# A hybrid layer on one core: second parts of weights on another engine, turns in another order, and another choice of places for expert weights

## The chip, the core and the metric

The kernel runs on one core of a Trainium2 chip. The metric is device time in microseconds (us), the median of several runs. The core has a matrix engine (PE), a vector engine (DVE), an activation engine (ACT), a general engine (POOL) and a queue (SP) from which nearly all transfers (DMAs) are issued. Each engine takes its instructions in the order in which the program holds them. The program here is a manual schedule: the order in which the Python code records instructions is the order on each engine, and a semaphore wait is put wherever one engine needs what another has made or must first have read.

## What is computed

One layer of a diffusion backbone over 512 latent tokens and 256 context tokens, width 1024, in float32. The reference, cut to its core:

```python
h  = modulate(rms_norm(x, w), shift, scale)         # also for the context tokens
u, q, k, v, ga, gb = split_in(h @ w_in)
ya = s5_mixer(uc, u)      # complex diagonal recurrence, both directions
yb = diff_attention(q, concat(kc, k), concat(vc, v))
m  = sigmoid(ga) * (ya @ w_proj_a) + sigmoid(gb) * (yb @ w_proj_b)
x  = x + g_m * rms_norm(m @ w_out, w_post)
h  = modulate(rms_norm(x, w_ffn), ...)
aff = softmax(h @ w_router); gates, idx = top_k(aff.T, 64)     # 16 experts, 64 tokens each
ys  = (silu(xs @ w_gate[e]) * (xs @ w_up[e])) @ w_down[e] * gates
x  = x + g_f * rms_norm(scatter_add(ys), w_post_ffn)
```

The weights of the 16 experts are 402.7 MB of the 467 MB that are moved.

## The kernel before

**Products in two parts.** In the layer's first part a float32 weight is split into two numbers that the PE takes at a higher rate: the first part is a rounded copy that ACT writes, the second part is weight minus first part (`lo`, L246). The PE adds three products per weight tile (`PASSES`): first by first, first by second, second by first. So the third matmul of a tile needs the second part. In the stretch of interest the second parts are subtractions of 128 x 1024 elements, and POOL makes them (`lo(GP, ...)`): by `parts` (L248 to 254) for the weights of u and v, by `prep_gate` (L662 to 671) for the gates ga.

**The recurrence.** The state-space branch runs over chunks. Its serial part is a loop of 95 steps on the DVE (L747 to 756), four small subtensor operations each (L753 to L756), recorded in one piece before any of the gates. While the DVE walks through it, the PE computes the eight gates ga (`gate`, L685; two halves of 12 matmuls each on 512 columns), after each half of gates 2 to 5 one group of "taps" (`taps`, L773: short convolution matrices, PE then ACT, into KS), and then v for the first six of eight weight tiles (`v_some`). Gate n+2's parts are made right after gate n, in one of two buffers (`wsp`); the raw weights come in pairs of gates (`load_gate`). When all taps are there, `mt_load` copies them by 30 small transfers from KS into MT, on the SP queue; behind them in the same queue stand the loads of the raw weights of v's tiles 2 and 3 (`fetch(vraw[p], 1536, p + 2)`). After v the PE computes the readout y (L865 on), which needs the recurrence's last states.

**Ahead of the recurrence** the DVE builds the state matrices (`matrices`, `state_make`, consumed by `ahead(n)`), the PE turns them (`state_turn`, L476), ACT copies the turned ones (WT, L491). The rows of u are turned by the DVE (`u_turn`, L558) through two buffers. Then the DVE builds the readout matrices (`cp_make`, four times five operations of 128 x 1024, L452 to L461).

**Places.** The memory for big tiles is a set of places of 128 x 2048 float32, handed out from a queue `E` (`take`, `give`). In the expert stage a load of 2 MB (`load_w`, L1617) takes from `E` either one whole place of 4096 columns (a pair: P0 to P5, and the first 4096 columns of SR) or two single ones (L places, SR's last part "SR1", and once each U2's and gm's). The P places lie where the front's weights lay, and come free with the last output projection (wo). `room` (L1604 to 1614) picks: the head of `E`; if that is a single one, also the next single one in the queue, wherever it stands. Since all loads go through SP in order, a load whose place is not yet free holds those behind it. An expert is twelve such loads: gate u0 to u3, up u0 to u3, down q0 to q3.

```python
tag = E.popleft()
if is_pair(tag):
    ...
tags = [tag, next(x for x in E if not is_pair(x))]
E.remove(tags[1])
```

Of the kernel before, what the change touches and what calls it, by code (L numbers as in the profile page):

```python
# [33 lines left out]
def layer(ctx: ExitStack, tc: tile.TileContext, A, out):  # L34
# [134 lines left out]
    def exp_exact(o, x, get):  # L169
        sh = list(x.shape)  # L170
        c, k, r, p, ki = get(*sh), get(*sh), get(*sh), get(*sh), get(*sh, dt=I32)
        V.tensor_scalar(c, x, -87.0, 88.0, op0=OP.max, op1=OP.min)
        V.tensor_scalar(k, c, 1.0 / math.log(2.0), MAGIC, op0=OP.mult, op1=OP.add)
        V.tensor_scalar(k, k, MAGIC, None, op0=OP.subtract)
        V.scalar_tensor_tensor(r, k, -LN2H, c, op0=OP.mult, op1=OP.add)
        V.scalar_tensor_tensor(r, k, -LN2L, r, op0=OP.mult, op1=OP.add)
        V.tensor_scalar(ki, k, 127.0, 8388608.0, op0=OP.add, op1=OP.mult)
        V.tensor_scalar(p, r, EXPC[0], None, op0=OP.mult)
        for a in EXPC[1:]:
            V.scalar_tensor_tensor(p, p, a, r, op0=OP.add, op1=OP.mult)  # L180
        V.scalar_tensor_tensor(o, p, 1.0, ki.bitcast(F32), op0=OP.add, op1=OP.mult)
# [63 lines left out]
    def lo(eng, o, a, hi):  # L245
        eng.tensor_tensor(o, a, hi.bitcast(F32), op=OP.subtract)  # L246

    def parts(raw, eng):  # L248

        t = take("wp")  # L250
        hi_, lo_ = t[:, 0:1024].bitcast(F32R), t[:, 1024:2048].bitcast(F32R)
        S.activation(hi_, raw, AF.Copy)
        lo(eng, lo_, raw, hi_)
        return t, [v.rearrange("p (k f) -> p k f", k=2) for v in (hi_, lo_)]

    PASSES = ((0, 0), (0, 1), (1, 0))
# [74 lines left out]
    S.activation(sc, th, AF.Sin)  # L331
    diagonals(0, 4, "rx")
    wu = [parts(wur[0], GP)]
    exp_exact(mag, q1, rowt)
    L = rowt(64, 4, 64)
    V.tensor_tensor(L[:, 0], mag, sc[:, 1], op=OP.mult)
    V.tensor_tensor(L[:, 1], mag, sc[:, 0], op=OP.mult)
    den, nr = rowt(64, 64), rowt(64, 64)
    V.tensor_tensor(den, lre, lre, op=OP.mult)
    V.tensor_tensor(q2, lim, lim, op=OP.mult)  # L340
    V.tensor_tensor(den, den, q2, op=OP.add)
    V.reciprocal(den, den)
    V.tensor_scalar(nr, L[:, 0], 1.0, None, op0=OP.subtract)
    V.tensor_tensor(q1, nr, lre, op=OP.mult)
    V.tensor_tensor(q2, L[:, 1], lim, op=OP.mult)
    V.tensor_tensor(q1, q1, q2, op=OP.add)
    V.tensor_tensor(L[:, 2], q1, den, op=OP.mult)
    V.tensor_tensor(q1, L[:, 1], lre, op=OP.mult)
    V.tensor_tensor(q2, nr, lim, op=OP.mult)
    V.tensor_tensor(q1, q1, q2, op=OP.subtract)  # L350
    V.tensor_tensor(L[:, 3], q1, den, op=OP.mult)
    pp = bank("prmT")
    PE.transpose(pp[:, 0:65], prm, ident[0:65, 0:65])
    prmT = keep.tile([128, 65], F32, name="prmT")

    for k in range(2):
        PE.transpose(pp[:, 128 + 12 * k:140 + 12 * k], prf[:, k::2], ident[0:12, 0:12])
    V.tensor_copy(prmT, pp[:, 0:65])
    prfT = keep.tile([128, 3, 8], F32, name="prfT")
    V.tensor_copy(prfT.rearrange("p v (u k) -> p k v u", k=2), pp[:, 128:152].rearrange("p (k v u) -> p k v u", k=2, v=3))  # L360

    def nb(t):

# [27 lines left out]
    ada_half(0)  # L391
    ada_mod(0)
    hh_ = [[take("hh") for _ in range(2)] for _ in range(2)]
    hh = [[hh_[r][d // 4][:, 512 * (d % 4):512 * (d % 4) + 512].bitcast(F32R) for d in range(8)] for r in range(2)]
    hc_ = [take("hc") for _ in range(2)]
# [230 lines left out]
    ub = ub_.rearrange("p (b g i h) -> p b g i h", b=2, g=G, i=2)  # L626
    u2 = big("U2", "u2").rearrange("p (g c) -> p g c", g=G)
    u_turn(2)
    ahead(4)
    u_turn(4)  # L630
    for kt in range(4, 8):
        u_some(range(2), kt)
    ahead(4)
    u_turn(0)
    give(*(w[0] for w in wu[2:]), ub_, xbc_)
    state_turn(0, 0)
    ahead(5)
    state_turn(1, 0)
    ahead(5)
    state_turn(0, 1)  # L640
# [7 lines left out]


    GW = {}  # L650

    def gate_room(raw):
        GW["raw"], GW["w"], GW["wv"] = raw, [], []
# [10 lines left out]
    def prep_gate(n, eng):  # L664
        if len(GW["w"]) < 2:
            GW["w"].append(take("wsp"))
            GW["wv"].append(GW["w"][-1].rearrange("p (r k f) -> p r k f", r=2, k=8).bitcast(F32R))
        w, c = GW["wv"][n % 2], 128 * (n % GW["k"])
        raw = GW["raw"].rearrange("p (k f) -> p k f", k=8)[:, :, c:c + 128]
        S.activation(w[:, 0], raw, AF.Copy)  # L670
        lo(eng, w[:, 1], raw, w[:, 0])

    def passes(ps, w, x, ks, last):
        for kt in ks:
# [5 lines left out]
    def gate(n, eng, get):  # L680

        sg = sga_ if n < 8 else sgb_
        if n % 4 == 0:
            sg.append(take("sg"))
        w = GW["wv"][n % 2]  # L685
        pg = get("gate")
        passes(pg, w, hh, range(4), 7)
        yield
        passes(pg, w, hh, range(4, 8), 7)
        S.activation(sg[-1][:, 512 * (n % 4):512 * (n % 4) + 512], pg, AF.Tanh, scale=0.5)  # L690
        if n % 8 < 6:
            prep_gate(n + 2, eng)
        if n < 8:
            if n in (1, 3):
                load_gate(n + 3)
        elif n < 13:
            load_gate(n + 3, 1)
        yield
# [2 lines left out]
    graw = take("graw")  # L701
    gate_room(graw)
    load_gate(0)
    prep_gate(0, GP)
    prep_gate(1, GP)
    load_gate(2)
    SR = big("SR", "SR").rearrange("p (c r g) -> p c r g", r=2, g=16)
    for dr in range(2):
        for gq in range(8):
# [14 lines left out]
    for dr in range(2):  # L724
        for gh in range(2):
            cp_make(dr, gh)
    give(mm)
    BZ_ = take("BZ")
    BZ = BZ_.rearrange("p (r g a h) -> p r g a h", r=2, g=32, a=2)
# [14 lines left out]
        cb = 97 + (31 - s if s < 32 else 127 - s)  # L744
        return SR[:, s:cb + 1:cb - s]

    for s in range(1, 96):  # L747
        if s == 32:
            V.tensor_copy(SR[:, 97 + 96], SR[:, 97])
        h0, h1 = rows(s - 1), rows(s)  # L750
        sp = keep.tile([128, 2, 2, 16], F32, name="sp", bufs=2)
        sq = keep.tile([128, 2, 2, 16], F32, name="sq", bufs=2)
        V.tensor_tensor(sp, h0, AR, op=OP.mult)  # L753
        V.tensor_tensor(sq, h0[:, :, ::-1], AI, op=OP.mult)  # L754
        V.tensor_tensor(sp, sp, h1, op=OP.add)
        V.tensor_tensor(h1, sp, sq, op=OP.add)  # L756


    co_ = [0]
# [51 lines left out]
    ft = taps()  # L811
    wv = []
    for n in range(8):
        if n == 7:
            wv += [parts(vraw[p], GP) for p in range(2)]
            for p in range(2):
                fetch(vraw[p], 1536, p + 2)
        for _ in gate(n, GP, cobank):
            if n > 1:
                next(ft, None)  # L820
        if n == 5:
            for _ in ft:
# [26 lines left out]
    for p in range(3):  # L849
        v_some(p, range(6))  # L850
        give(wv[p][0])
        if p < 2:
            wv.append(parts(vraw[p % 2], GP))
    give(vraw_)


    YS_ = take("YS")
# [745 lines left out]

    def room():  # L1604

        tag = E.popleft()
        if is_pair(tag):
            t = wl[:, 0:4096] if tag[0] == "SR" else pr.tile([128, 4096], F32, name="we", tag="P%d" % tag[1])
            return t, [t[:, 0:2048], t[:, 2048:4096]], [tag]
        tags = [tag, next(x for x in E if not is_pair(x))]  # L1610
        E.remove(tags[1])
        return None, [regs.tile([128, 2048], F32, name="wh", tag=x) if isinstance(x, str) else wl[:, 4096:6144] if x[0] == "SR" else
                      gm_ if x[0] == "gm" else yp_.rearrange("p b d -> p (b d)") for x in tags], tags

    def done_w(tags):
        E.extend(x for x in tags if x[0] not in ("U2", "gm"))
# [231 lines left out]
```

## Time and profile before

| | us |
|---|---|
| median of 3 runs | 1612.13 (1611.4 to 1614.61) |
| the profiled execution's own time | 1610.17 |
| its span, first to last instruction | 1608.4 |
| PE busy | 1394.9 (87%) |
| DVE busy | 553.9 (34%) |
| ACT busy | 292.6 (18%) |
| POOL busy | 173.9 (11%) |
| HBM read | 461.66 MB, 288 GB/s over the span |

Busy shares are averages over two unlike stages: the front (to about 640 us), where all engines take part, and the experts (from there on), where PE and transfers run side by side. The chain of waits (part 4 of the profile's page) is followed back from the last instruction; a row of a timeline gives start, length, engine, line, operation, output and inputs, and in brackets how long the engine had stood idle before it and what ended that.

### The profile page before, as it was taken

What the parts mean: (1) busy time and instruction counts of PE and PEld (TensorE: products, weight loads), DVE (VectorE), ACT (ScalarE), POOL (GpSimd) and SP (SyncE); (2) the same over time, 40 slices, a digit from 0 to 9 for tenths busy, and PEclk for the clock granted to TensorE, in tenths of its full rate; (3) what the DMA queues carried; (4) which work ended last, traced back from release to release, by engine and by line L of the source; (5) the groups of instructions that cost most, each with busy time, mean ns of one, the idle gap of its engine ahead of it and who ended that gap; (6) DMA issues with size and microseconds to landing.
All of it is one profiled execution on the core that took longest, in us unless ns stands there. A gap on an engine that the chain in (4) does not pass through costs nothing.

```text
span 1608.4 us, 17710 instructions
## 1 busy us (share of the span) xinstructions
PE 1394.9 (87%) x7230; PEld 745.4 (46%) x7230; DVE 553.9 (34%) x1363; ACT 292.6 (18%) x566; POOL 173.9 (11%) x115
## 2 busy tenths in 40 slices
PE   5989959996997894989988979988989979989984
PEld 3778746874664583424324324324324324324322
DVE  6789952276656637001102102102002002012003
ACT  3572104145442331100000000000000000000002
POOL 2123302443123300000000000000000000000003
PEclk9999979998997896999999999999999999999998
DMA  9112402322444157389999999999999999999994
GB/s 331 38 54 83 76 27 96 92 92 86 154 181 157 34 190 318 127 373 426 426 427 427 426 427 428 425 427 427 427 427 426 427 426 427 428 427 428 426 413 159
DMA packets 76881, 467.01 MB, mean 290 GB/s; under 512 B 13716, under 2 KB 33360, under 8 KB 46432
## 3 DMA queue, kind: packets, MB, share of 16 engines
q1 hardware_dynamic: 75616, 463.62, 71.6%
q10 hardware_dynamic: 768, 2.13, 0.3%
q8 instruction: 57, 0.93, 0.2%
q0 software_dynamic: 416, 0.12, 0.0%
q14 instruction: 24, 0.20, 0.0%
HBM read 461.66 MB, written 2.10 MB: 288 GB/s over the span
## 4 chain that ended last, share of the span: by engine, by line
PE 47%; DMA 30%; DVE 17%; ACT 3%; issue 2%; POOL 0%; SPq 0%; DVEq 0%; ACTq 0%
DMA we<-in_w_exp_up_dram 18%; DMA we<-in_w_exp_down_dram 11%; PE gu L1673 11%; PE yd L1705 8%; PE gat L1643 4%; PE sca L1717 4%; PE wo L1520 3%; PE gate L676 2%; DVE SR L756 2%; PE u L548 2%; DVE sp L753 1%; PE k L1054 1%; PE proj L676 1%; DVE sq L754 1%; PE y L877 1%
## 5 line engine op out<-in xcount | busy, mean ns | idle before, releaser
L1673 PE MATMUL gu<-we,gm 128*64 128x512 f32 x752 | 169.5, 600 | 23.3 <-DMA we<-in_w_exp_up_dram 20.1
L1673 PE MATMUL gu<-we,gf 128*64 128x512 f32 x752 | 169.1, 600 | 22.8 <-DMA we<-in_w_exp_up_dram 18.3
L1684 DVE TENSOR_TENSOR hid<-hid,gu 128x512 f32<-128x512 f32 x32 | 21.9, 688 | 481.1 <-PE gu L1673 481.1
L1705 PE MATMUL yd<-we,hid 128*64 128x512 f32 x688 | 152.9, 595 | 9.4 <-DMA we<-in_w_exp_down_dram 9.4
L1758 POOL TENSOR_TENSOR fin<-facc,gf 128x256 f32<-128x256 f32 (+1 forms) x12 | 10.6, 914 | 1020.0 <-DMA we<-in_w_exp_down_dram 1015.8
L1673 PEld LDWEIGHTS gu<-we,gm 128*64 128x64 f32 x752 | 53.0, 138 | 138.1 <-issue 105.8
L1673 PEld LDWEIGHTS gu<-we,gf 128*64 128x64 f32 x752 | 53.1, 138 | 136.7 <-issue 104.9
L676 PE MATMUL gate<-hh,wsp 128*128 128x512 f32 x384 | 95.8, 403 | 12.4 <-ACT sg L690 12.0
L1705 PEld LDWEIGHTS yd<-we,hid 128*64 128x64 f32 x688 | 48.6, 137 | 106.6 <-issue 91.3
L1710 DVE COPY mo<-yd 64x512 f32<-64x512 f32 x15 | 10.4, 694 | 227.8 <-ACT mo L1709 227.8
L676 PEld LDWEIGHTS gate<-hh,wsp 128*128 128x128 f32 x384 | 71.9, 192 | 29.1 <-ACT sg L690 12.4
L1643 PE MATMUL gat<-mo,x 128*128 128x128 f32 x512 | 71.8, 300 | 10.2 <-DVE mo L1635 10.2
L1643 PEld LDWEIGHTS gat<-mo,x 128*128 128x128 f32 x512 | 67.3, 208 | 18.3 <-issue 15.2
L1681 ACT ACTIVATE hid<-gu 128x512 f32<-128x512 f32 x32 | 19.1, 597 | 297.8 <-PE gu L1673 297.8
L1717 PE MATMUL sca<-mo,gm 128*128 128x512 f32 (+1 forms) x136 | 61.6, 591 | 4.8 <-ACT mo L1709 4.8
L1689 ACT COPY hid<-ht 128x512 f32<-128x512 f32 x16 | 9.4, 587 | 270.5 <-PE ht L1688 270.5
L1520 PE MATMUL wo<-wo,mp 128*128 128x512 f32 x192 | 47.5, 404 | 2.3 <-DVE at L1380 2.3
L1709 ACT ACTIVATE mo<-yd 64x512 f32<-64x512 f32 x15 | 8.9, 590 | 219.0 <-PE yd L1705 219.0
L1722 DVE TENSOR_TENSOR facc<-facc,sca 128x512 f32<-128x512 f32 (+1 forms) x60 | 38.6, 651 | 18.8 <-PE sca L1717 18.7
L1673 PE MATMUL gu<-wl,gm 128*64 128x512 f32 x200 | 45.0, 599 | 0.0
L1717 PEld LDWEIGHTS sca<-mo,gm 128*128 128x128 f32 x136 | 21.5, 188 | 44.4 <-DVE facc L1722 23.6
L1520 PEld LDWEIGHTS wo<-wo,mp 128*128 128x128 f32 x192 | 36.6, 194 | 10.4 <-DVE at L1380 2.8
(439 smaller groups left out, 1985.2 us busy)
## 6 DMA issues: line engine op xcount, KB each, us to landing
we<-in_w_exp_up_dram SPq DMA_DIRECT2D x48, 2048.0 KB, 32.6
we<-in_w_exp_gate_dram SPq DMA_DIRECT2D x46, 2048.0 KB, 34.2
we<-in_w_exp_down_dram SPq DMA_DIRECT2D x43, 2048.0 KB, 26.7
wl<-in_w_exp_gate_dram SPq DMA_DIRECT2D x9, 2048.0 KB, 29.9
araw<-in_w_ada_dram SPq DMA_DIRECT2D x16, 1024.0 KB, 6.3
wl<-in_w_exp_down_dram SPq DMA_DIRECT2D x7, 2048.0 KB, 33.8
wl<-in_w_exp_up_dram SPq DMA_DIRECT2D x7, 2048.0 KB, 26.7
wl<-in_w_exp_down_dram SPq DMA_DIRECT2D x11, 1024.0 KB, 31.9
```

The costliest lines, as they stand in the source:

```text
L548: PE.matmul(ps, tok(a, i, kt), w[b][:, kt % 2], start=kt == first and n == 0, stop=kt == last and n == 2)
L676: PE.matmul(ps, w[:, a, kt], x[b][kt], start=kt == 0 and n == 0, stop=kt == last and n == 2)
L753: V.tensor_tensor(sp, h0, AR, op=OP.mult)
L756: V.tensor_tensor(h1, sp, sq, op=OP.add)
L1520: PE.matmul(po[j], mparts(a, kt)[:, 128 * i:128 * i + 128], wo[kt][:, D * b + 512 * j:D * b + 512 * j + 512].bitcast(F32R), start=kt == 0 ...
L1643: PE.matmul(pg, x1[i][:, nb(d)], oh[:, i].rearrange("p e s -> p (e s)"), start=i == 0, stop=i == 3)
L1673: PE.matmul(pq[b][64 * j:64 * j + 64], xst[e // 2 % 2][:, kt, e % 2], wv[:, c:c + 512], start=kt == 0, stop=kt == 7, skip_group_check=True)
L1681: S.activation(hid[0][:, 1 - e % 2, b], pq[b], AF.Silu)
L1684: V.tensor_tensor(act, act, pgu[1][b], op=OP.mult)
L1705: PE.matmul(py[64 * j:64 * j + 64], hT_[:, b, i, 64 * jf:64 * jf + 64], wv[:, c:c + 512], start=(q == 0 and i == 0), stop=(q == 3 and i == ...
L1717: PE.matmul(po, gm[:, g0:g0 + 128], yp_[:, ep % 2, c], start=True, stop=True)
L1722: V.tensor_tensor(dst, dst, po, op=OP.add)
```

## The change

Four edits. (1) `prep_gate` and `parts` take `None` for the engine: the subtraction then goes into a list `due`, and `second_parts()` records what is in it, on the DVE. The recurrence becomes a generator; `steps(n)` records n of its steps, and the code calls it four steps per half of a gate and ten per tile of v, with `second_parts()` in between. The loads of raw gate weights that must follow a subtraction go into the same list. The fetch of v's raw tiles 2 and 3 moves behind gate 7. (2) `u_turn(4)` stands ahead of the state matrices' next four pieces, and the first state turn ahead of `u_turn(0)`. (3) In the setup the first half of the modulation (`ada_half(0)`, `ada_mod(0)`) stands ahead of the DVE's work on the discretisation, and two small copies go from the DVE to ACT. (4) `room` walks `E` and takes what is complete first: a pair, or the second of two single places.

```diff
         S.activation(hi_, raw, AF.Copy)
-        lo(eng, lo_, raw, hi_)
+        if eng is None:
+            due.append(lambda: lo(V, lo_, raw, hi_))
+        else:
+            lo(eng, lo_, raw, hi_)
...
     u_turn(2)
+    u_turn(4)
     ahead(4)
-    u_turn(4)
     for kt in range(4, 8):
         u_some(range(2), kt)
-    ahead(4)
+    state_turn(0, 0)
+    ahead(2)
     u_turn(0)
     give(*(w[0] for w in wu[2:]), ub_, xbc_)
-    state_turn(0, 0)
-    ahead(5)
+    ahead(7)
...
             if n in (1, 3):
-                load_gate(n + 3)
+                due.append(lambda: load_gate(n + 3))
...
-    prep_gate(0, GP)
-    prep_gate(1, GP)
-    load_gate(2)
+    prep_gate(0, None)
+    prep_gate(1, None)
+    due.append(lambda: load_gate(2))
...
         for gh in range(2):
             cp_make(dr, gh)
+        second_parts()
...
     for n in range(8):
         if n == 7:
-            wv += [parts(vraw[p], GP) for p in range(2)]
+            wv += [parts(vraw[p], None) for p in range(2)]
+        for half, _ in enumerate(gate(n, None, cobank)):
+            steps(4)
+            if half == 0:
+                second_parts()
+            if n > 1:
+                next(ft, None)
+        if n == 7:
             for p in range(2):
                 fetch(vraw[p], 1536, p + 2)
-        for _ in gate(n, GP, cobank):
-            if n > 1:
-                next(ft, None)
...
         if p < 2:
-            wv.append(parts(vraw[p % 2], GP))
+            wv.append(parts(vraw[p % 2], None))
+        steps(5)
+        second_parts()
+        steps(5)
     give(vraw_)
+    steps(95)
...
-        tag = E.popleft()
-        if is_pair(tag):
...
-        tags = [tag, next(x for x in E if not is_pair(x))]
-        E.remove(tags[1])
+        ones_ = []
+        for tag in E:
+            if is_pair(tag):
+                E.remove(tag)
...
+            ones_.append(tag)
+            if len(ones_) == 2:
+                break
```

**On the general engine and the vector engine.** During the first gates POOL's row was this (wsp: a gate's two parts, at gates 2 to 4 here; KS: the taps):

```order
L730 MEMSET BZ 128x2048
L768 TENSOR_TENSOR cn<-ident 32x16
L769 TENSOR_TENSOR cn<-cn,DG 32x256
L246 TENSOR_TENSOR wsp<-graw,wsp 128x1024 x2
L797 TENSOR_TENSOR KS<-KS,cn 32x4x16
L246 TENSOR_TENSOR wsp<-graw,wsp 128x1024
L797 TENSOR_TENSOR KS<-KS,cn 32x4x16 x2
```

It is now the following, and POOL's next subtraction is the one for the readout's gate (wg):

```order
L744 MEMSET BZ 128x2048
L790 TENSOR_TENSOR cn<-ident 32x16
L791 TENSOR_TENSOR cn<-cn,DG 32x256
L819 TENSOR_TENSOR KS<-KS,cn 32x4x16 x4
L246 TENSOR_TENSOR wg<-wgr,wg 128x2048
```

The DVE has the twelve subtractions: those of gates 0 and 1 together between the second and the third `cp_make`, gate 2's behind step 12 of the recurrence, those of gates 3 to 7 behind every eighth step after it, those of v's tiles 0 and 1 behind step 60, tile 2's behind step 69, tile 3's behind step 79. Tile 2's place, in the middle of the steps:

```order
L771 TENSOR_TENSOR SR<-sp,sq 128x2x32
L246 TENSOR_TENSOR wp<-vraw,wp 128x1024
L768 TENSOR_TENSOR sp<-SR,AR 128x64
L769 TENSOR_TENSOR sq<-SR,AI 128x64
L770 TENSOR_TENSOR sp<-sp,SR 128x64
```

What moved: the 26 steps behind it, and all that the DVE does after, now stand behind that one subtraction.

**On the SP queue, the first expert.** Before (wh: a single place; wl: SR's, 4096 the whole pair, 2048 its last part; mo: U2's; we: a P place):

```order
L1626 DMA wh<-in_w_exp_gate_dram 128x2048 x3
L1626 DMA mo<-in_w_exp_gate_dram 128x2048
L1623 DMA wl<-in_w_exp_gate_dram 128x4096
L1623 DMA we<-in_w_exp_gate_dram 128x4096
L1623 DMA we<-in_w_exp_up_dram 128x4096 x4
L1623 DMA we<-in_w_exp_down_dram 128x4096
L1626 DMA wl<-in_w_exp_down_dram 128x2048
L1626 DMA gm<-in_w_exp_down_dram 128x2048
L1626 DMA wh<-in_w_exp_down_dram 128x2048 x3
L1626 DMA wl<-in_w_exp_down_dram 128x2048
L1623 DMA wl<-in_w_exp_gate_dram 128x4096
```

Now:

```order
L1661 DMA wh<-in_w_exp_gate_dram 128x2048 x2
L1658 DMA wl<-in_w_exp_gate_dram 128x4096
L1661 DMA mo<-in_w_exp_gate_dram 128x2048
L1661 DMA wh<-in_w_exp_gate_dram 128x2048
L1658 DMA we<-in_w_exp_gate_dram 128x4096
L1658 DMA we<-in_w_exp_up_dram 128x4096 x4
L1658 DMA we<-in_w_exp_down_dram 128x4096
L1661 DMA wl<-in_w_exp_down_dram 128x2048
L1661 DMA gm<-in_w_exp_down_dram 128x2048
L1661 DMA wh<-in_w_exp_down_dram 128x2048 x2
L1658 DMA wl<-in_w_exp_down_dram 128x4096
L1658 DMA we<-in_w_exp_gate_dram 128x4096 x4
```

What moved: the first expert's down q3 was a single place and SR1, which that expert's own q1 fills; it is now the SR pair, which holds gate u1. And because the changed order of `take` and `give` in the front leaves other L places free, the second half of gate u2 now lies in a place (L3) that wo still reads, where it lay in one that was free earlier.

## Rows read from the trace of the kernel before

**Rows 1.** The page: its span, and part 2, transfers in 40 slices
```profile
span 1608.4 us, 17710 instructions
...
DMA  9112402322444157389999999999999999999994
```
**Rows 2.** The page, part 4: the chain that ended last, by engine
```profile
PE 47%; DMA 30%; DVE 17%; ACT 3%; issue 2%; POOL 0%; SPq 0%; DVEq 0%; ACTq 0%
```
**Rows 3.** Stretches of 10 us: length, busy time by engine, PEclk, DMA share, GB/s
```profile
650.00:660.00 10.00, 10.00 (x58) 5.37 (x58) 0.47 (x2) 0.92 (x2) 0.00 (x0) 1.00 0.56 231
...
680.00:690.00 10.00, 9.87 (x50) 3.93 (x50) 1.54 (x3) 0.59 (x1) 0.00 (x0) 1.00 0.18 45
...
750.00:760.00 10.00, 9.77 (x46) 3.02 (x42) 0.00 (x0) 0.18 (x1) 0.00 (x0) 1.00 1.00 428
```
**Rows 4.** Timeline of the SP queue, 540 to 760 us
```profile
611.77 0.33 SPq L1623 DMA_DIRECT2D we<-in_w_exp_gate_dram  x1
...
640.27 9.84 SPq L1626 DMA_DIRECT2D wh<-in_w_exp_down_dram  x3
687.18 0.33 SPq L1626 DMA_DIRECT2D wl<-in_w_exp_down_dram  x1
```
**Rows 5.** The SP queue's waits: total, times, longest
```profile
SPq L1626 <- PE yd L1705: 126.8, 14, 37.0
```
**Rows 6.** Timeline of the PE, first expert
```profile
653.82 1.94 PE L1673 MATMUL gu<-mo,gf 128*64 128x512 f32 x8
...
662.84 17.39 PE L1673 MATMUL gu<-we,gf 128*64 128x512 f32 x80
```
**Rows 7.** The PE's waits, 640 to 1575 us: total, times, longest
```profile
PE gu L1673 <- DMA we<-in_w_exp_up_dram: 38.4, 29, 2.3
```
**Rows 8.** Timeline of the DVE, start of two steps of the recurrence
```profile
132.03 0.23 DVE L753 TENSOR_TENSOR sp<-SR,AR 128x64 f32<-128x64 f32 x1
...
132.82 0.22 DVE L753 TENSOR_TENSOR sp<-SR,AR 128x64 f32<-128x64 f32 x1
```
**Rows 9.** Line L756, the last operation of each step: ns least/median/most, first and last start
```profile
L756 DVE TENSOR_TENSOR SR<-sp,sq x95: 224/225/2469, 129.6 to 223.9; 128x64 f32<-128x64 f32 x95
```
**Rows 10.** Groups by line, 100 to 240 us: POOL's subtractions for gates
```profile
L246 POOL TENSOR_TENSOR wsp<-graw,wsp 128x1024 fp32r<-128x1024 f32 x8 | 21.5, 2692 | 68.0 <-ACT wsp L670 53.7 <-PE K L790 14.3
```
**Rows 11.** Timeline of the DVE, readout matrices
```profile
99.74 1.23 DVE L456 TENSOR_TENSOR CP<-mm 128x1024 f32<-128x1024 f32 x1
...
105.98 3.27 DVE L456 TENSOR_TENSOR CP<-mm 128x1024 f32<-128x1024 f32 x1
...
125.53 3.30 DVE L461 TENSOR_TENSOR CP<-mm 128x1024 f32<-128x1024 f32 x1
```
**Rows 12.** Timeline of the PE: gate 2's second half, gate 6, the readout's start
```profile
133.20 3.01 PE L676 MATMUL gate<-hh,wsp 128*128 128x512 f32 x12
...
168.40 11.17 PE L676 MATMUL gate<-hh,wsp 128*128 128x512 f32 x48
...
223.36 1.98 PE L877 MATMUL y<-CP,SR 64*64 64x128 f32 x16 [16.97 <-DVE SR L756]
...
228.36 1.17 PE L877 MATMUL y<-CP,SR 64*64 64x128 f32 x16
```
**Rows 13.** Stretches of 5 us, columns as in rows 3
```profile
215.00:220.00 5.00, 0.00 (x0) 0.00 (x0) 4.55 (x27) 0.00 (x0) 0.00 (x0) 0.50 0.00 2
```
**Rows 14.** Timeline of the SP queue: the loads of v's raw tiles 2 and 3
```profile
189.16 1.80 SPq L242 DMA_DIRECT2D vraw<-in_w_in_dram  x2
```
**Rows 15.** Timeline of ACT: first part of v's tile 2; u's last turn
```profile
91.18 1.09 ACT L562 ACTIVATE U<-u 128x512 f32<-128x512 f32 x2 [5.60 <-DVE u L563]
...
194.21 1.06 ACT L252 ACTIVATE wp<-vraw 128x1024 fp32r<-128x1024 f32 x1 [14.01 <-DMA vraw<-in_w_in_dram]
```
**Rows 16.** Timeline of the PE: the first normalised tile
```profile
27.43 2.05 PE L406 MATMUL xT<-early,xs 128*128 128x128 f32 x8 [2.27 <-DVE prfT L360]
29.41 1.12 PE L569 MATMUL LT<-ident,rowt 64*64 64x64 f32 x16
```

More of the change, by code (lines that the diff above doesn't have):

```diff
@@ L333, in layer @@
     wu = [parts(wur[0], GP)]
[L334 to L351, printed above, removed]
     pp = bank("prmT")
@@ L357, in layer @@
         PE.transpose(pp[:, 128 + 12 * k:140 + 12 * k], prf[:, k::2], ident[0:12, 0:12])
-    V.tensor_copy(prmT, pp[:, 0:65])
+    S.copy(prmT, pp[:, 0:65])
     prfT = keep.tile([128, 3, 8], F32, name="prfT")
-    V.tensor_copy(prfT.rearrange("p v (u k) -> p k v u", k=2), pp[:, 128:152].rearrange("p (k v u) -> p k v u", k=2, v=3))
+    S.copy(prfT.rearrange("p v (u k) -> p k v u", k=2), pp[:, 128:152].rearrange("p (k v u) -> p k v u", k=2, v=3))
+    exp_exact(mag, q1, rowt)
     def nb(t):
@@ L392, in layer @@
     ada_mod(0)
+    L = rowt(64, 4, 64)
+    V.tensor_tensor(L[:, 0], mag, sc[:, 1], op=OP.mult)
+    V.tensor_tensor(L[:, 1], mag, sc[:, 0], op=OP.mult)
+    den, nr = rowt(64, 64), rowt(64, 64)
+    V.tensor_tensor(den, lre, lre, op=OP.mult)
+    V.tensor_tensor(q2, lim, lim, op=OP.mult)
+    V.tensor_tensor(den, den, q2, op=OP.add)
+    V.reciprocal(den, den)
+    V.tensor_scalar(nr, L[:, 0], 1.0, None, op0=OP.subtract)
+    V.tensor_tensor(q1, nr, lre, op=OP.mult)
+    V.tensor_tensor(q2, L[:, 1], lim, op=OP.mult)
+    V.tensor_tensor(q1, q1, q2, op=OP.add)
+    V.tensor_tensor(L[:, 2], q1, den, op=OP.mult)
+    V.tensor_tensor(q1, L[:, 1], lre, op=OP.mult)
+    V.tensor_tensor(q2, nr, lim, op=OP.mult)
+    V.tensor_tensor(q1, q1, q2, op=OP.subtract)
+    V.tensor_tensor(L[:, 3], q1, den, op=OP.mult)
     hh_ = [[take("hh") for _ in range(2)] for _ in range(2)]
@@ L650, in layer, with second_parts @@
     GW = {}
+    due = deque()
+    def second_parts():
+        while due:
+            due.popleft()()
     def gate_room(raw):
@@ L670, in prep_gate @@
         S.activation(w[:, 0], raw, AF.Copy)
-        lo(eng, w[:, 1], raw, w[:, 0])
+        if eng is None:
+            due.append(lambda: lo(V, w[:, 1], raw, w[:, 0]))
+        else:
+            lo(eng, w[:, 1], raw, w[:, 0])
     def passes(ps, w, x, ks, last):
@@ L745, in rows, with scan, steps @@
         return SR[:, s:cb + 1:cb - s]
[L747 to L756, printed above, removed]
+    def scan():
+        for s in range(1, 96):
+            if s == 32:
+                V.tensor_copy(SR[:, 97 + 96], SR[:, 97])
+            h0, h1 = rows(s - 1), rows(s)
+            sp = keep.tile([128, 2, 2, 16], F32, name="sp", bufs=2)
+            sq = keep.tile([128, 2, 2, 16], F32, name="sq", bufs=2)
+            V.tensor_tensor(sp, h0, AR, op=OP.mult)
+            V.tensor_tensor(sq, h0[:, :, ::-1], AI, op=OP.mult)
+            V.tensor_tensor(sp, sp, h1, op=OP.add)
+            V.tensor_tensor(h1, sp, sq, op=OP.add)
+            yield
+    fscan = scan()
+    def steps(n):
+        for _ in range(n):
+            next(fscan, None)
     co_ = [0]
@@ L1604, in room @@
     def room():
-        tag = E.popleft()
-        if is_pair(tag):
-            t = wl[:, 0:4096] if tag[0] == "SR" else pr.tile([128, 4096], F32, name="we", tag="P%d" % tag[1])
-            return t, [t[:, 0:2048], t[:, 2048:4096]], [tag]
-        tags = [tag, next(x for x in E if not is_pair(x))]
-        E.remove(tags[1])
+        ones_ = []
+        for tag in E:
+            if is_pair(tag):
+                E.remove(tag)
+                t = wl[:, 0:4096] if tag[0] == "SR" else pr.tile([128, 4096], F32, name="we", tag="P%d" % tag[1])
+                return t, [t[:, 0:2048], t[:, 2048:4096]], [tag]
+            ones_.append(tag)
+            if len(ones_) == 2:
+                break
+        for tag in ones_:
+            E.remove(tag)
         return None, [regs.tile([128, 2048], F32, name="wh", tag=x) if isinstance(x, str) else wl[:, 4096:6144] if x[0] == "SR" else
-                      gm_ if x[0] == "gm" else yp_.rearrange("p b d -> p (b d)") for x in tags], tags
+                      gm_ if x[0] == "gm" else yp_.rearrange("p b d -> p (b d)") for x in ones_], ones_
     def done_w(tags):
```

## The prediction

> **What bounds the kernel now.** The page comes first. Its transfer line [rows 1] splits the program: from about 690 us on the 16 transfer engines are full up to the last stretch, before that they are not. The chain [rows 2] names PE and DMA first and gives the DVE 17%, nearly all of it in the front. So two questions decide: when does the full stream begin, and what ends last in the front, which everything behind it follows.
>
> The stream, by stretches of 10 us [rows 3]: at 750 us 428 GB/s, the level of every stretch after it, so 2 MB take 4.9 us and 1 MB 2.45 us. But from 650 to 660 only 0.56 of the stretch is used, and from 680 to 690 only 0.18. That hole runs from 655.6 to about 688.2 us, 32.6 us. The SP queue shows why [rows 4]: after three issues from 640.27 to 650.1 the next comes at 687.18, and its wait is the longest of its line, 37.0 us on yd, the down product [rows 5]. It is the first expert's own down product: down q3 stands behind SR1, which q1 fills. All loads behind it are held too. Against this the PE waits for up weights only 38.4 us in all from 640 to 1575 us [rows 7], its largest wait for a transfer: it is close behind the stream but not its bound.
>
> The front: a step of the recurrence takes 0.79 us (132.03 to 132.82) [rows 8], so 95 want 75 us. The last operations of the first and the 95th step start at 129.6 and 223.9 us [rows 9], 94.3 us for 94 steps, where 74.3 would do. Row 9's most, 2469 ns against a median of 225, says where 20 us go: single operations of the DVE held while POOL subtracts. Eight such subtractions of gates lie here and just before it, 2.69 us each [rows 10]. The PE stands idle 16.97 us until the recurrence lets the readout start at 223.36 [rows 12].
>
> **The change, part by part**, on the profiled execution's clock (1610.17 us, 2.0 below the median of 1612.13; I take differences here and set them against the median).
>
> *Start of the recurrence.* The second parts of gates 0, 1 and 2 lengthened three DVE operations from 1.23 to about 3.3 us [rows 11] (the third, at 109.29, is like the one at 105.98): 3 x 2.05 = 6.2 us go. Two subtractions come to the DVE. Its own price for two inputs of 128 x 1024 is 1.23 us [rows 11], with the gap 1.25: 2.5 us. The setup edit saves some 0.2 us: the first normalised tile waits 2.27 us for a small copy [rows 16], and may start that much sooner, but the matmuls LT behind it in the PE's queue need the DVE's discretisation, now later, so nearly all is given back at 29.4. Bounds: 0 to 2.3 us; I take 0.2, as LT stands in the PE's order ahead of all that follows. The turn edit takes away ACT's wait of 5.60 us for a buffer [rows 15] and lets gate 0 start about 3.4 us sooner; the DVE's row of operations is as long as before, so the recurrence gets nothing. Start: 129.1 - 6.2 + 2.5 - 0.2 = 125.2 us.
>
> *Gate 2.* The gain of the turns is lost at once: gate 2's second part now stands behind 12 steps, and is ready at 125.2 + 12 x 0.79 + 1.25 = 136.0 us, while gate 2 could begin at 133.20 - 3.0 - 2.7 - 3.4 = 124.1 (second half's start, a half, the first taps, the turns' gain). The PE stands still for some 11 us; in the like pause before the readout the granted clock fell to 0.50 [rows 13], the lower level of 1.2 GHz, and two groups of 16 matmuls took 1.98 us where later ones take 1.17 [rows 12]: 1.6 us for the return. The third matmul, the first that needs the second part, went at about 128.0 and now goes at 136.0; with the return the gate is 9.6 us late. Later gates come in time: a round of eight steps and a subtraction is 7.6 us of DVE, a gate with taps (168.40 - 133.20) / 3.5 = 10.1 us of PE [rows 12]. So the taps end at 168.4 + 9.6 = 178.0 us.
>
> *Tiles 2 and 3 of v.* Behind the taps 28 of mt_load's transfers leave one by one, and then the raw tiles: issue at 189.16 [rows 14], first landing at 194.21 [rows 15], which is 25.8 us after the taps' end. Before, POOL and ACT waited there, and nobody minded. Now the DVE waits: it reaches tile 2's subtraction at about 195 us (125.2 + 69 x 0.79 + 8 x 1.25 + 5.3, my estimate of short waits for ACT's first parts), but the tile lands at 178.0 + 25.8 = 203.8; ACT takes 1.06 [rows 15], the DVE 1.25. From 206.1 on 26 steps (20.5) and tile 3 (1.25) are left: the recurrence ends at 227.9 us, not 224.1. The front is **3.8 us longer**, though 12 subtractions are gone from POOL. Bounds: with no loss at gate 2 the DVE's own sum ends it, 125.2 + 75.1 + 10 x 1.25 + 5.3 = 218.1, 6 us shorter; with a return to full clock twice as dear and one raw load late by 2 us, 7 us longer. I stay near the upper half because the waits stand in the order itself. That the DVE cannot pass over the waiting subtraction is the order's reading; the Trainium skill (TensorE: Matmul & The Clock Gate, its opening table) calls the VectorE's queue strictly first in, first out; no run here shows the wait yet. If the queue could pass over it, the front would be that of rival (a).
>
> *Places.* Loads move 1 MB from before the issue at 611.77 [rows 4] to behind it (L3, read until then by wo): 2.5 us lost. Then down q3 goes to the SR pair, free when the PE has done gate u1's four products, 653.82 + 1.94 = 655.8 [rows 6]: data from 656.8 to 661.7. The next load needs P0, free when gate u3 is read: two of ten parts of 1.74 us from 662.84, so 666.3 [rows 6], data from 667.3. From there the PE frees 2 MB each 3.5 us and a load takes 4.9: full. The hole shrinks from 32.6 to 1.3 + 5.6 = 6.9 us, a gain of 25.7 - 2.5 = **23.2 us**. It stays a gain only while transfers bound the end. The stream takes 24 x 4.9 = 118 us per pair of experts; the PE's waits for up weights alone are 38.4 / 8 = 4.8 us per pair [rows 7], so it needs 113 at most. Filling the hole puts it some 16 us behind the stream at first, which it makes up at 4.8 us a pair or faster, within the eight pairs. Bounds: 0 (the PE takes over) and 32.6 (no hole); I take 23.2, and 18 to 27 as its own spread. The end of the stream keeps its order of places.
>
> Sum: 3.8 - 23.2 = -19.4; 1612.1 - 19.4 = **1592.7 us**.
>
> **Rivals.** (a) *The recurrence does gain*: the PE does not lose at gate 2 what I say, the raw tiles come in time, the front is 6 us shorter. For it: 20 us of holding go [rows 9]; against it: 25.8 us from the taps to the tile. 1612.1 - 23.2 - 6.0 = 1582.9. (b) *POOL and DVE trade evenly*: holding removed equals subtractions added and waits; front unchanged, 1588.9. Row 10 speaks against: 2.69 us there, 1.23 here. The Trainium skill (Perfetto Trace Analysis, Optimizing Scalar/DVE Operations) says that moving operations between these two engines might not help, as they share a read port. (c) *The PE takes over as bound* once the hole is filled, and only its waits of the first pair are gained, three of the longest, 2.3 us [rows 7], so 7: 1612.1 - 7 + 3.8 = 1608.9. For it: 38.4 us of waits are little [rows 7]; against: they recur in every expert (29 times), so the PE is faster in each. (d) *Slower: PE and DVE take turns*. If each second part is made only after the gate before has ended, gates 2 to 5 take 10.1 + 7.6 = 17.7 us each from 135 us on, the taps end at 205.8, the recurrence 49.9 us later at 255.7, 31.6 us late: 1612.1 - 23.2 + 31.6 = 1620.5. It decides from where a DVE round exceeds a PE round; 7.6 against 10.1, and two buffers, speak against it. (e) *The places do nothing*: some other load stands in the way in the same hole. Only the front's loss is left: 1615.9.
>
> **How the numbers follow.** Forecast 0.58, (a) 0.17, (b) 0.08, (c) 0.10, (d) 0.04, (e) 0.03. The forecast's own range is 1586 to 1601 (front +1 to +7, stream 18 to 27). To leave out no more than two in ten I reach down past (a) to 1581 and to 1602 above; (c) to (e) stay outside. A measurement can tell 0.2%, 3.2 us: faster is forecast, (a), (b) and most of (c), 0.90; the same, the rest of (c), 0.03; slower, (d) and (e), 0.07.
>
> **What would show it.** Right: no DVE operation of the recurrence above 0.4 us; gate 2's third matmul waiting for the DVE until about 136 us, granted clock low there; a DVE wait of some 9 us before tile 2's subtraction, ended by ACT; readout at about 227. Transfers full from 667 + 4 us on but for a hole of 5 or 6 us before it, no SP wait of 37 us; PE waits for transfers only from the third or fourth pair. Wrong: the readout before 222, or a second hole in the stream between 690 and 900, which would say that the places come free too late.

## The result: 1594.16 us, and where the time went

The changed kernel takes 1594.16 us (median of 4 runs, 1590.99 to 1597.17), the kernel before 1612.18: a ratio of 0.9885, with a 95% interval of 0.9863 to 0.9908. The forecast was 1592.7, its range 1581 to 1602.

The page of the changed kernel, its span, the transfers in 40 slices and the chain by engine, beside [rows 1, 2]:

```profile
span 1589.2 us, 17706 instructions
...
DMA  9110512222453156799999999999999999999994
...
PE 53%; DMA 23%; DVE 12%; ACT 2%; SPq 2%; issue 1%; POOL 0%; DVEq 0%; ACTq 0%
```

In the 17th slice of the transfers, 636 to 675 us here and 643 to 684 before, a 7 stands where a 3 stood; the chain has lost DVE and DMA and gained PE.

Three points on the SP queue cut each execution into a front (up to the first load of the projection, issued right behind the readout), a middle (up to the load of the first expert's down q2 into an L place, `wh`, the first down load that has to wait for its place) and the stream. The timeline of the SP queue of the changed kernel has all three, and the two issues after them, beside [rows 4]:

```profile
249.97 1.19 SPq L942 DMA_DIRECT2D px<-in_w_proj_a_dram  x2
...
641.90 6.91 SPq L1661 DMA_DIRECT2D wh<-in_w_exp_down_dram  x2
657.50 0.33 SPq L1658 DMA_DIRECT2D wl<-in_w_exp_down_dram  x1
668.23 10.63 SPq L1658 DMA_DIRECT2D we<-in_w_exp_gate_dram  x4
```

Before, these points lie at 248.68, 640.27 and 1608.4. So the front is 1.3 us longer, the middle 0.3 longer (391.9 against 391.6), the stream 20.8 shorter (947.3 against 968.1). Where SP stood 37.0 us [rows 5] it now issues at 657.50 and 668.23; the forecast had 655.8 and 666.3, which are 657.4 and 667.9 here, where the middle ends 1.6 us later than before.

The stream, by stretches of 10 us (columns as in [rows 3]):

```profile
650.00:660.00 10.00, 10.00 (x56) 4.79 (x52) 0.44 (x2) 0.91 (x2) 0.00 (x0) 1.00 0.67 247
660.00:670.00 10.00, 10.00 (x54) 4.44 (x52) 0.41 (x1) 2.93 (x4) 0.00 (x0) 1.00 0.53 187
670.00:680.00 10.00, 10.00 (x48) 3.30 (x46) 0.00 (x0) 0.00 (x0) 0.00 (x0) 1.00 0.96 405
760.00:770.00 10.00, 10.00 (x34) 3.12 (x34) 4.51 (x7) 0.00 (x0) 0.00 (x0) 1.00 0.91 374
```

The last row is a small loss that before did not have: at 757 to 769 us SP waits 11.6 us for the PE to read a gate part. Counted in bytes from the issue of the down load that begins the stream, in stretches of 10 us against a full 428 GB/s, before lacks 33.8 us of stream, after 10.7 and 2.2 more in this dip. The difference, 20.9, is the stream's gain.

The front of the changed kernel. The last operation of each step of the recurrence, beside [rows 9]:

```profile
L771 DVE TENSOR_TENSOR SR<-sp,sq x95: 224/225/227, 124.0 to 224.9; 128x64 f32<-128x64 f32 x95
```

No operation is stretched any more (most 227 ns, before 2469), and the first step is 5.6 us earlier; yet the last ends 1 us later. Waits took the rest. The PE at gate 2's third matmul, at its second half, and at the readout, with the wait before it in brackets, beside [rows 12]:

```profile
134.07 4.34 PE L689 MATMUL gate<-hh,wsp 128*128 128x512 f32 x10 [12.77 <-DVE wsp L246]
...
141.01 2.99 PE L689 MATMUL gate<-hh,wsp 128*128 128x512 f32 x12
...
224.35 1.98 PE L907 MATMUL y<-CP,SR 64*64 64x128 f32 x16 [11.16 <-DVE SR L771]
```

And the DVE, ahead of tile 2's second part, and the next step's first operation behind it (the step before ended at 192.91):

```profile
202.45 1.22 DVE L246 TENSOR_TENSOR wp<-vraw,wp 128x1024 fp32r<-128x1024 f32 x1 [9.55 <-ACT wp L252]
203.59 0.22 DVE L768 TENSOR_TENSOR sp<-SR,AR 128x64 f32<-128x64 f32 x1
```

The DVE does nothing for 9.55 us although the next steps, which need nothing of tile 2, stand behind the subtraction. ACT's first part, which it waits for, waited 13.37 us for the raw tile; that was issued at 196.66 us, when MT's 30 transfers were through. Four shorter waits of the DVE, for ACT's first parts of gates 4 to 7, make another 6.1 us.

### The profile page after: what moved, and what is told of

Its sections match the earlier page's. It is cut to its first block, busy times and chain, and to the rows that moved or that the text cites. A ratio compares the mean times of both kernels' runs of the same rounds, so it can differ in the third digit from the quotient of the medians.

```text
span 1589.2 us, 17706 instructions
## 1 busy us (share of the span) xinstructions
PE 1388.3 (87%) x7230; PEld 748.7 (47%) x7230; DVE 540.4 (34%) x1373; ACT 291.7 (18%) x568; POOL 143.3 (9%) x103
## 4 chain that ended last, share of the span: by engine, by line
PE 53%; DMA 23%; DVE 12%; ACT 2%; SPq 2%; issue 1%; POOL 0%; DVEq 0%; ACTq 0%
PE gu L1708 14%; DMA we<-in_w_exp_up_dram 13%; PE yd L1740 9%; DMA we<-in_w_exp_down_dram 9%; PE gat L1678 5%; PE gate L689 4%; PE sca L1752 4%; PE wo L1550 3%; PE k L1084 1%; PE proj L689 1%; PE y L907 1%; PE o L1260 1%; PE s L1222 1%; PE ada L1167 1%; PE K L812 1%
## 5 line engine op out<-in xcount | busy, mean ns | idle before, releaser
L689 PE MATMUL gate<-hh,wsp 128*128 128x512 f32 x384 | 99.3, 413 | 25.2 <-DVE wsp L246 12.8
L1678 PE MATMUL gat<-mo,x 128*128 128x128 f32 x512 | 76.5, 313 | 10.2 <-DVE mo L1670 10.2
L1678 PEld LDWEIGHTS gat<-mo,x 128*128 128x128 f32 x512 | 71.9, 221 | 18.3 <-issue 15.2
L1708 PE MATMUL gu<-wl,gm 128*64 128x512 f32 x208 | 48.5, 610 | 3.1 <-DMA wl<-in_w_exp_up_dram 3.1
L1740 PE MATMUL yd<-wl,hid 128*64 128x512 f32 x192 | 44.4, 596 | 0.0
```

What stands on the lines that cost most here:

```text
L689: PE.matmul(ps, w[:, a, kt], x[b][kt], start=kt == 0 and n == 0, stop=kt == last and n == 2)
L1678: PE.matmul(pg, x1[i][:, nb(d)], oh[:, i].rearrange("p e s -> p (e s)"), start=i == 0, stop=i == 3)
L1708: PE.matmul(pq[b][64 * j:64 * j + 64], xst[e // 2 % 2][:, kt, e % 2], wv[:, c:c + 512], start=kt == 0, stop=kt == 7, skip_group_check=True)
L1740: PE.matmul(py[64 * j:64 * j + 64], hT_[:, b, i, 64 * jf:64 * jf + 64], wv[:, c:c + 512], start=(q == 0 and i == 0), stop=(q == 3 and i == ...
```

## The experiments

Ten kernels were run: edits alone (e1, e2, e6 to e8), then the two long waits taken away (e3 the DVE's at tile 2, e4 the PE's at gate 2), then what is left (e5, e9, e10).

**e1_places**: the kernel before with the new `room()` alone.

> The kernel before with the new choice of places alone. Theory (the stream's gain stands by itself and adds to the front's): the front stays where it was (readout at 223 to 224 us), the hole in the stream shrinks from 32.6 to about 8 us, and the 1 MB that the whole change loads later (L3) is not late here, because before still lists L0; so some 23 us less than before, 1589 us. Rival (the places work only together with the new front): less than 12 us gained, above 1600. Rival (PE becomes the bound once the hole is filled): about 7 us gained, 1605.

1593.34 us, a ratio of 0.9881 (0.9864 to 0.9897). In its profile the front is 248.3 us, as before, and the stream 947.4, as in the changed kernel. The middle, whose code is untouched, took 395.8 instead of 391.6: that is why it is not at 1589 (more on it below). The stream's gain stands by itself, and both rivals fall. L3's late megabyte costs nothing either: with it (after, 947.3) and without (e1, 947.4) the stream is equally long. The changed kernel issues it at 606.59 us, into a stretch without transfers.

**e2_front**: the changed kernel with the old `room()`.

> The changed kernel with the old choice of places: second parts between the steps, setup and turns, but no place out of turn. Theory (this part costs a little): the front 1.5 to 2 us later than before, the wait of SP for the down product stays at 35 to 37 us; L3's late 1 MB is swallowed by that hole, whose end the PE sets; 1613.5 to 1614.5. Rival a (the recurrence gains 6 us): 1606. Rival (L3's 2.5 us and the front's add): 1616.

1614.80 us, 1.0016 (1.0004 to 1.0027). The front is 250.6 us, 2.0 longer than before, SP's wait is 37.0 us again and the stream 967.4. That is 0.3 us above what was expected. So the other three edits together cost about 2 us, and rival a, a gain of the recurrence, did not happen. 2.3 us here and 19.2 gained in e1 make 16.9 gained together, where the whole change has 18.0.

**e6_pool**: the second parts back on POOL, everything else of the change kept.

```
-    prep_gate(0, None)
-    prep_gate(1, None)
+    prep_gate(0, GP)
+    prep_gate(1, GP)
...
-        for half, _ in enumerate(gate(n, None, cobank)):
+        for half, _ in enumerate(gate(n, GP, cobank)):
...
-            wv += [parts(vraw[p], None) for p in range(2)]
+            wv += [parts(vraw[p], GP) for p in range(2)]
```

(and the same for tiles 2 and 3 of v.)

> The changed kernel with all second parts back on POOL (first edit undone; setup, turns and places stay). Theory (moving them to the DVE gained at the start, 6.2 us of holding, and lost more at gate 2 and tile 2, so that by itself it is about even or a small loss here): DVE operations of 2.4 us and more come back among the steps, the 95th step ends at 222 to 224, the first load of the projection is issued at 247 to 249 instead of 250.0, from the down load's issue to the end still 947 us; 1590 to 1593. Rival (the move itself is the front's gain and something else cost it): the 95th step ends later than 226, 1596 or more.

1590.50 us, 0.9866 (0.9840 to 0.9893). The steps, by the same line as above:

```profile
L771 DVE TENSOR_TENSOR SR<-sp,sq x95: 224/225/2295, 131.0 to 222.8; 128x64 f32<-128x64 f32 x95
```

The held operations are back and the steps begin 7 us later than in the changed kernel, yet they end 2 us sooner; the front is 248.1 us against 250.0 (250.6 in e2, which has the changed kernel's front). So the move of the second parts to the DVE, the change's first and largest edit, costs 1.9 to 2.5 us of front in the place where it was put: 7 us gained at the start, 9 lost behind it, where 15.6 us of waits and ten subtractions outweigh the operations that POOL held. It is read from one profile each; the medians' intervals overlap.

**e3_mt_late**: MT's transfers behind the raw tiles 2 and 3.

```
             for p in range(2):
                 fetch(vraw[p], 1536, p + 2)
+            mt_load()
+            give(KS_)
         if n == 5:
...
-            mt_load()
-            give(KS_)
```

> The changed kernel with the 30 transfers of MT behind the raw tiles 2 and 3 of v instead of ahead of them. Theory (the DVE waits for tile 2 because its load stands behind MT's transfers): the raw tile is issued at about 186 instead of 196.7 us, the DVE's wait of 9.5 us before tile 2's second part falls under 2, the 95th step ends at about 216 instead of 225, PE's wait before the readout falls from 11.2 to 2 to 4 us, and the kernel takes about 1585.5. Rival (MT becomes what the readout waits for): readout 220 or later, waiting for DMA, 1590 or more. Rival (time gained in the front is lost before the stream begins): readout at 216 but 1593 to 1594.

1580.74 us, 0.9805 (0.9789 to 0.9822). The raw tiles' issue, from the SP queue's timeline:

```profile
187.49 1.50 SPq L242 DMA_DIRECT2D vraw<-in_w_in_dram  x2
```

and the readout's start, from the PE's:

```profile
217.41 1.17 PE L907 MATMUL y<-CP,SR 64*64 64x128 f32 x16 [1.54 <-DVE SR L771]
```

9.2 us earlier the one, 6.9 the other; the DVE's wait before tile 2 is gone from its list of waits, and the front is 240.7 us, 9.3 less. The steps end at 218.1, not 216, as they began 1.9 us later in this execution. The readout's first 16 matmuls take 1.17 us where they took 1.98: the PE had waited 1.54 us only, and the granted clock had not fallen. The theory holds; the medians differ by 13.4 us where the profiled spans differ by 9.6, as the changed kernel's profiled run was its fastest.

**e4_gate2_early**: each gate's second part ahead of the steps. As gate 0 now has no steps and each half of the others five, tile 2's subtraction also moves, from behind step 69 to behind step 75.

```
         for half, _ in enumerate(gate(n, None, cobank)):
-            steps(4)
             if half == 0:
                 second_parts()
+            steps(5 if n else 0)
```

> The changed kernel with gate 2's second part made before the first step, and each later one ahead of its gate's first steps (no steps in gate 0, then five each half). Theory: PE's wait of 12.8 us at gate 2 falls under 2, the clock does not fall there, the taps end at 162 to 165 instead of 176 us, tile 2 is issued at about 184 and the DVE waits for it under 3 us; the steps end at 215 to 218, the readout starts there; about 1585.5. Rival (gate 2's wait costs nothing since the recurrence ends the front): taps earlier but steps still ending at 223 to 225, 1593 to 1594. Rival (the DVE now waits for ACT's first part in every gate instead): steps end at 222 or later.

1578.26 us, 0.9789 (0.9772 to 0.9805). The PE at gate 2 and at the readout:

```profile
125.34 4.13 PE L689 MATMUL gate<-hh,wsp 128*128 128x512 f32 x10 [3.50 <-DVE wsp L246]
...
210.89 1.98 PE L907 MATMUL y<-CP,SR 64*64 64x128 f32 x16 [6.58 <-DVE SR L771]
```

The wait fell to 3.50 us, not under 2 (the DVE still has the readout's matrices in front), the granted clock still fell (0.66 from 125 to 130 us), and the taps end at 167.4 rather than 162 to 165. But the raw tiles are issued at 188.0, the DVE waits 1.5 us for tile 2, and the steps end at 211.6: sooner than the 215 to 218 expected, since with the gates' waits gone too the DVE has hardly a gap. The six more steps ahead of tile 2 have a part in it: the DVE comes to that subtraction at 192.2 us with 75 steps done, and with 69, at 0.79 us a step, it would have waited some 6.2 us there instead of 1.5 (an estimate). The rival, that gate 2's wait costs nothing, falls: it delayed the taps, the taps MT's transfers, these the raw tile, and that the steps, as the marks of this run and of e3 show.

**e10_tile3_last**: e4 with tile 3's second part after the last step.

```
-        second_parts()
+        if p == 0:
+            second_parts()
         steps(5)
-    give(vraw_)
     steps(95)
+    second_parts()
+    give(vraw_)
```

> The kernel of e4_gate2_early with the second part of v's tile 3, which is multiplied only behind the readout, made after the last step. Theory (the DVE's row of steps and subtractions is without a gap, so its sum sets the readout): the 95th step ends 1.2 us sooner, 210.1 to 210.7, the readout at 209.5 to 210.2; 1576.5 to 1577.5, which the runs can hardly tell from 1578.3. Rival (something else ends there): step 95 within 0.5 us of 211.6.

```profile
L771 DVE TENSOR_TENSOR SR<-sp,sq x95: 224/225/227, 125.5 to 210.3; 128x64 f32<-128x64 f32 x95
```

The last operation starts at 210.3, where e4's starts at 211.4: 1.1 us, of which 0.2 is an earlier start of the steps, and the rest about one subtraction. The DVE's sum sets the readout there. 1576.66 us, 0.9772 (0.9758 to 0.9787), the fastest of all, though its interval overlaps e4's.

**e9_pool_v**: e4 with the four second parts of v's tiles on POOL.

> The kernel of e4_gate2_early with the four second parts of v's tiles on POOL again, the gates' six staying on the DVE: the price of an operation held by POOL against one done by the DVE, where nothing else waits. Theory (a POOL subtraction holds the DVE about 2.05 us, its own takes 1.25): the 95th step ends 4 x 0.8 = 3.2 us later than 211.6, at 214.5 to 215.2, the readout's start and the projection's first load later by the same; 1581 to 1582. Rival (they trade evenly, one port between them): step 95 within 0.7 us of 211.6.

The DVE's timeline where POOL makes the part of tile 0, one of four such places:

```profile
175.50 2.34 DVE L771 TENSOR_TENSOR SR<-sp,sq 128x64 f32<-128x64 f32 x1
```

Each POOL subtraction (2.39 us) stretches one operation of the DVE by 2.1 us; the same subtraction on the DVE took 1.22, and the operation behind it started 1.14 after it. The last step ends at 214.8, 3.2 us later than in e4. That is the expected figure, but partly by chance: the steps begin 0.7 us later here, and e4 has a wait of 1.5 us before tile 2 that e9 has not. From the first step's last operation to the 95th's it is 88.1 us against 85.7, and 84.2 without that wait, so four subtractions on POOL cost the steps 3.9 us more than four on the DVE, 1.0 each. The front is 239.4 us against 235.5. Of this the median shows little: 1579.33 us, 0.979 (0.9775 to 0.9805), not the 1581 to 1582 expected. Its middle happened to be 2.4 us shorter than e4's. The rival, an even trade, falls where the DVE's row has no gaps.

**e5_fill**: e4 with half of v's last tile ahead of the readout.

```
+    v_some(3, range(3))
     for gq in range(4):
         readout(gq)
...
     channels(0)
-    v_some(3, range(3))
     channels(1)
```

> The kernel of e4_gate2_early with the first half of v's last tile (18 matmuls, 7 us) ahead of the readout instead of behind it, to fill PE's wait of 6.6 us. Theory (the DVE's own sum, 95 steps and 10 subtractions, sets the readout's start, and PE's idle time there also costs clock): the wait falls under 1 us, no matmul of the readout takes longer than 1.2 us a group of 16 from the first on, the readout ends 1.5 to 2.5 us sooner, and the glu products 3 to 5 us sooner; 1573 to 1575.5. Rival (ACT's copies and Gelu behind the readout set the glu): the readout ends sooner, the glu does not; 1577 to 1578.

1579.89 us, 0.9792 (0.9772 to 0.9812): nothing gained. The PE behind the readout:

```profile
240.45 1.34 PE L969 MATMUL yT<-ident,YS 128*128 128x128 f32 x8 [2.44 <-ACT yg L972]
```

The wait before the readout fell from 6.6 to 2.4 us, but the readout's first group still takes 1.97 us, and behind the readout the PE now waits for ACT. The matmuls that follow the readout (`glu`) start 0.8 us sooner than in e4, not 3 to 5. The 18 matmuls filled 4.5 us, not 7, and the steps ended 1.0 us later in this execution. The rival was right that ACT sets the glu; that the readout ends sooner, which both had, did not come: its last matmuls end at 236.6 us, 235.5 in e4.

**e7_setup** and **e8_turns**: the kernel before with one of the two small edits.

> The kernel before with the setup edit alone (small copies on ACT, the adaptive half ahead of the discretisation). Theory (it is this edit, not the turns, that let the steps start 1.7 us sooner than forecast): LT's four groups run between the DVE's quarters, the first step's end comes 1.0 to 1.6 us sooner than 129.6 and the readout too; gate 0 up to 1.5 us sooner than 116.7; about 1610 to 1613. Rival (the discretisation, now behind, delays LT by what the tile gains): first step within 0.3 us of 129.6.

> The kernel before with the turns edit alone. Theory (PE's states come sooner, the DVE's row of operations is as long as before): gate 0 starts 4 to 7 us sooner than 116.7, the first step's end within 0.5 us of 129.6, the readout too, the time within 0.2% of before. Rival (the turns let the steps start sooner): first step's end 1 us or more before 129.6.

The start of gate 0, from the PE's timeline of e7 and then of e8:

```profile
115.72 9.61 PE L677 MATMUL gate<-hh,wsp 128*128 128x512 f32 x41 [0.46 <-ACT SR L722]
```

```profile
111.16 13.94 PE L676 MATMUL gate<-hh,wsp 128*128 128x512 f32 x60 [0.48 <-ACT SR L721]
```

1.0 and 5.5 us sooner than the 116.7 of before, as both expectations had it; 7.1 together in the changed kernel. The fronts are 248.7 and 247.4 us, against 248.7; one run each took 1611.70 and 1612.04 us, no change that can be told. The first step's end says nothing here: it came 2 us *later* in both (131.6 and 131.5 us), because POOL's subtraction for gate 3, which held that very operation at 129.65 us before, came sooner and held an operation ahead of the steps instead, while the steps still end 0.3 to 0.5 us sooner. Both expectations named the wrong place to look. A better one is the DVE's first operation for the readout matrices (`cn`, L645 of the kernel before), ahead of all that POOL holds there: it starts at 96.59 us before, 96.66 in e1, 96.38 in e7 and 96.67 in e8. So neither edit by itself moves the DVE by more than 0.3 us. In the changed kernel it starts at 95.08, but at 96.32 in e2 and 96.95 in e3, whose instructions up to there are the same: the 1.7 us by which the changed kernel's steps start before the forecast are no more than what executions of one front differ by.

All profiles, cut at the same three points (us):

| kernel | places | front | middle | stream | last step ends |
|---|---|---|---|---|---|
| before | old | 248.7 | 391.6 | 968.1 | 224.1 |
| e2 | old | 250.6 | 394.7 | 967.4 | 226.8 |
| e7 | old | 248.7 | 392.2 | 969.0 | 223.8 |
| e8 | old | 247.4 | 394.8 | 968.1 | 223.6 |
| after | new | 250.0 | 391.9 | 947.3 | 225.1 |
| e1 | new | 248.3 | 395.8 | 947.4 | 223.7 |
| e6 | new | 248.1 | 393.1 | 948.0 | 223.0 |
| e3 | new | 240.7 | 391.9 | 947.0 | 218.1 |
| e4 | new | 235.5 | 394.0 | 947.3 | 211.6 |
| e5 | new | 236.6 | 391.4 | 946.9 | 212.6 |
| e9 | new | 239.4 | 391.6 | 946.9 | 214.8 |
| e10 | new | 234.9 | 392.2 | 947.3 | 210.6 |

The stream has two lengths, 968.1 (mean of 4) and 947.3 (mean of 8), whatever the front: the places are worth 20.9 us, and in the profiled spans a microsecond of front goes through to the end, apart from the middle's own changes.

## Why the prediction was right, step by step

*Places.* Right in mechanism, 2.3 us too much in size: 23.2 forecast, 20.9 measured. The hole itself gave what was said, by the byte count 33.8 less 10.7, 23.1 us, but that is partly luck. The working had a remaining hole of 6.9 us and 2.5 us lost for L3's megabyte. That load leaves at 606.59 us, ahead of gate u3's at 613.51, and loses nothing; e1, which does not have it, has no smaller hole (11.6 us by the same count). The megabyte that is missing ahead of the hole is another, which the working overlooked: the first half of down q3 stood there as the last of three loads (`wh` x3 in [rows 4]) and now goes with its second half to the SR pair behind (`wh` x2). So the transfers run dry 41.2 us after gate u3's issue, 43.7 before. Also the two loads that interrupt the hole start slowly, at 229 GB/s from 658 to 660 us and at 229 and 246 in the two microseconds from 669 on, where the working had the full rate. What was priced at nothing is the 2.2 us lost at about 768 to 772 us, nearly the whole difference: once the hole is filled, the transfers have caught up with the PE, and a place comes late. A second hole between 690 and 900 was among the prediction's signs of being wrong; it came, small. Rival (c), the PE as the bound, was present for that dip only. The sign named for it came out nearly: waits of the PE for transfers were to come from the third or fourth pair of experts on; from 640 to 860 us its list has none, and the first are these, from 860 to 880 (total, times, longest), at the end of the second pair:

```profile
PE gu L1708 <- DMA we<-in_w_exp_up_dram: 2.0, 2, 1.2
```

*Start of the recurrence.* Forecast 125.2 us, measured 123.45, but 124.70 in e2 and 125.33 in e3 with the same instructions ahead of it: right, within what executions differ by. The setup edit's 0.2 us came out on the DVE (e7, 0.2 to 0.3), though not by the reason given. The prediction let the matmuls LT, and all behind them, wait for the whole discretisation; they run from 26.2 us on in e7, half of them ahead of it, where they began at 29.4 [rows 16]. It is the PE that gains by it: gate 0 comes 1.0 us sooner in e7.

*Gate 2.* Forecast: second part ready at 136.0 us, second half at 142.8, taps' end at 178.0, granted clock 0.50. Measured: 134.07 (wait 12.77), 141.01, 176.2, and 0.50 from 125 to 135 us, here in the first of the two stretches:

```profile
125.00:130.00 5.00, 0.00 (x0) 0.00 (x0) 4.56 (x26) 0.00 (x0) 0.00 (x0) 0.50 0.00 0
```

All of it is 1.8 us early by the earlier start. That this wait costs what it was said to is shown by e4: without most of it the taps end 8.9 us sooner.

*Tiles 2 and 3 of v.* Forecast 25.8 us from the taps' end to ACT's part, and a DVE wait of some 9 us; measured 25.1 and 9.55. e3 shows the cause: move MT's transfers and the wait is gone. The 5.3 us that the prediction put down for short waits for ACT's first parts, without a row for them, measured 6.1.

*The front's sum.* Forecast +3.8, measured +1.3 (+1.0 at the last step), and in e2, which has the same front, +2.0 (+2.7): some 2 us too much loss, the larger part of it in the changed kernel's profile the early start of that execution. e6 and e2 agree that the three edits ahead of the places gain nothing. That the DVE does not pass over a waiting subtraction, which no run of before could show, is now seen in the trace, as the Trainium skill has it (TensorE: Matmul & The Clock Gate, opening table): 9.55 us idle in front of steps that were ready. Had it been otherwise, the front would have come near rival (a)'s.

*Rival (b)*, an even trade of POOL and DVE, came out in the total (the front is level within 1.9 us in e6), but not for its reason: with no wait beside it, a subtraction costs the steps 2.1 us on POOL and 1.1 on the DVE (e9). The advice of the Trainium skill (Perfetto Trace Analysis, Optimizing Scalar/DVE Operations) that such a move might not help held here because of what the moved work waits for, not because of the read port that it names: in e9 against e4 the move by itself gains 1.0 us a subtraction. Rival (d) fell: from gate 3 on the gates came in time, as 7.6 against 10.1 us said.

*The sum.* -19.4 forecast, -18.0 between the medians, -19.2 between the profiled spans. Two errors of opposite sign, 2.3 us too much on the stream and 2.5 too much loss in the front (1.8 against e2), make it look better than its parts were.

## What to carry to other kernels

Work that is moved onto an engine that runs a serial chain costs not only its own time but every wait of its inputs: place it where its input is surely there (behind a landed load, ahead of the steps that don't need it), or the chain stands. Here that order was worth 14 to 15 us (e4, e10), more than the choice of engine. And a queue of loads that is issued in order should take next the place that comes free next, not the one that is first in a list; after such a hole is filled, look for the next place that comes late, since the consumer is then the bound for a while.

## What was not expected of the hardware

The middle, whose instructions are the same in all kernels but e5, took from 391.6 to 395.8 us, more than several of the effects measured here. Part of it lies in how long the same matmuls are busy: the middle's 1654 matmuls take 331.5 us in the kernel before, whose middle is 391.6 us, and 336.1 in e1, whose middle is 395.8, at a mean granted clock of 0.91 and 0.90. But this is not the whole account: in e9 they take 334.0 us, and its middle is 391.6 too. Why the clock falls at other moments there from one execution to the next, and what else sets the middle's length, was not tried and stays open. For effects of 1 to 3 us the timeline's marks within one stretch told more than the medians of whole runs, though they too have their spread: with the same instructions ahead of it, the recurrence's first step starts anywhere between 123.45 and 125.33 us in three profiles.
